# Down products of a seven-product block multiplication in another order, with partial sums left in PSUM

## The chip, the cores and the metric

The kernel runs on one core of one Trainium2 chip. The time is device microseconds of one execution: 2502.7 us, the median of three runs (2497.94 to 2503.45).

## The reference

Two request groups of 1024 tokens pass through the same one-layer trunk, with shared weights, one group ("trunk 0", "trunk 1") after the other. All inputs and outputs are float32.

```python
xn = rms_norm(h, norm_mix_g[l])
proj = xn @ w_in[l]                       # attention and recurrent branch
...
h = h + jnp.concatenate([attn_o, lru_o], axis=-1) @ w_out[l]
xn = rms_norm(h, norm_ffn_g[l])
g, u = jnp.split(xn @ w_gate_up[l], 2, axis=-1)
h = h + (jax.nn.silu(g) * u) @ w_down[l]  # hidden 2816, model 1024
h = rms_norm(h, final_norm_g)
```

The change is in how `(silu(g) * u) @ w_down` is computed and added to `h`.

## The kernel before

**Seven products.** The down product is a 2x2 block multiplication done with seven block products instead of eight. A[i,j] are blocks of the activation: i is the parity of a block of 128 tokens, j the parity of a block of 128 hidden channels. B[j,l] are blocks of `w_down`: j as above, l the half of the 1024 output columns. Each product P1 to P7 multiplies a sum of A blocks by a sum of B blocks; each result goes, with a sign, into one or more of the four blocks (i,l) of the residual `h`, by the table `C`.

**Phases and chunks.** The order of products is the tuple `DN` (L36). A product runs over NC = 11 chunks c of 256 hidden channels; here a product with its 11 chunks is called a phase, and one chunk a unit. `dn_unit` (L1933) issues a unit's matmuls: for four groups q of 128 token pairs, three matmuls of 128x512 (`mm3`, L428), since each float32 operand is split into a high and a low part. So a unit has 12 matmuls, a phase 132, the down stage of a trunk 77 units and 924 matmuls, all on TensorE (PE). The four results of a phase lie in four PSUM banks; two sets of four alternate (`bank(n % 2, ...)`). When a phase is over, its additions into `h` (VectorE, DVE, one bank and one block each) are queued and issued between the matmuls of the next phase, evenly; in P3, two to a unit.

**Preparing a unit.** `prep_dn` (L1717) forms the sums of A and B in place on DVE or GpSimd (POOL), and ScalarE (ACT) then writes the high parts of both operands, `sop` from A and `top` from B. `prep_dn_lo` (L1755) writes the low parts, that of B on DVE, that of A on POOL. Operand tiles come from a ring of seven (`wop` in profile and order). `prep` (L1780) is called ahead of each unit: it prepares units so that at most three are out, and `lows` writes the low parts of this unit and the next. Each engine works its own instructions in the order in which they are issued.

**Where the data is.** The A blocks are stored to DRAM (`ad`) by the gate-up stage and come back by `a_load` in the hook of the last gate-up tile (`gu_hook`, L1883), into the tiles aA, aB, aC, aD, aS and aV. Tile aA and parts of aB hold the block of the first phase. aC holds A[2,2] and aD A[2,1], eight of 11 chunks in one DMA of 2 MB each; the other three chunks of each lie in aB and aS. The same hook loads `h` (eight DMAs of 512 KB) and the tiles `trun` (blocks B[1,1], all 11 chunks). All other B blocks come as pieces `wraw` through a ring of four slots: the list `items` (from L1641) gives their order, and `load` (L1655) issues item i only once the units of item i-4 have been prepared (`freed`). All of these DMAs are issued by SyncE (SP), one after the other, in program order, and each waits for its slot to be free and for an earlier DMA.

Of the kernel before, what the change touches and what calls it, by code (L numbers as in the profile page):

```python
# [12 lines left out]
ALU = mybir.AluOpType  # L13
# [3 lines left out]
P = 128  # L17
# [15 lines left out]


GU = (("P1", "B11"), ("P6", "T2"), ("P2", "B21"), ("P7", "T3"), ("P5", "T1"), ("P4", "T4"), ("P3", "B22"))
DN = ("P1", "P2", "P4", "P5", "P7", "P6", "P3")  # L36
NC = NHT // 2

GELU_A = 0.044715
# [205 lines left out]
def hymba_kernel(ctx, tc, ins, outs, dbg=None):  # L245
# [1366 lines left out]
    def ffn_stream(T, b):  # L1612
# [10 lines left out]
        raws = {}  # L1623
# [3 lines left out]
        A = T.A = {}  # L1627

        def rows(t, cs, n=1):
            return wdn[t * P:(t + n) * P, cs]  # L1630
# [10 lines left out]
        def two(p, j, cs):  # L1641
            for c in range(0, NC, 2):
                items.append(((p, c), [P, 2, 512], [
                    (lambda r, i=i: r[:, i], rows(2 * (c + i) + j, cs)) for i in range(min(2, NC - c))]))

        two("P2", 1, L0)
        for c in range(NC):
            items.append((("P4", c), [P, 2, 512], [(lambda r, i=i: r[:, i], rows(2 * c + i, L1)) for i in range(2)]))
        for c in range(NC):
            items.append((("P5", c), [P, 2, 512], [(lambda r: r.rearrange("p a b -> p (a b)"), rows(2 * c, slice(0, D)))]))  # L1650
        two("P6", 0, L0)
        two("P3", 1, L1)
        freed = set()

# [61 lines left out]

        def prep_dn(p, c):  # L1717
            tr = trun[c // 2][:, c % 2]
            turn = (dve, pool)[c % 2]
            if p == "P1":  # L1720
                src, s = tr, A[1, 1, c]
            elif p == "P2":
                src, s = raws[(p, c - c % 2)][:, c % 2], A[1, 2, c]
                dve.tensor_tensor(tr, tr, src, ALU.subtract)
            elif p == "P4":
                r = raws[(p, c)]
                b12, b22 = r[:, 0], r[:, 1]
                dve.tensor_tensor(b22, b22, b12, ALU.subtract)
                turn.tensor_tensor(b12, b22, tr, ALU.add)
                src, s = b12, A[2, 2, c]  # L1730
            elif p == "P5":
                r = raws[(p, c)]
                dve.tensor_tensor(A[2, 2, c], A[2, 1, c], A[2, 2, c], ALU.add)
                dve.tensor_tensor(r[:, 0], r[:, 1], r[:, 0], ALU.subtract)
                src, s = r[:, 0], A[2, 2, c]
            elif p == "P7":
                dve.tensor_tensor(A[2, 1, c], A[1, 1, c], A[2, 1, c], ALU.subtract)
                src, s = tr, A[2, 1, c]
                dve.tensor_tensor(A[1, 1, c], A[2, 2, c], A[1, 1, c], ALU.subtract)
            elif p == "P6":  # L1740
                r = raws[(p, c - c % 2)]
                dve.tensor_tensor(tr, tr, r[:, c % 2], ALU.add)
                src, s = tr, A[1, 1, c]
            else:
                src, s = raws[(p, c - c % 2)][:, c % 2], A[1, 2, c]
            sop, top = op_tile(), op_tile()
            act.copy(sop[:, 0], s)
            act.copy(top[:, 0], src)
            if p == "P4":
                act.copy(tr, r[:, 1])  # L1750
            if p == "P6":
                turn.tensor_tensor(A[1, 2, c], A[1, 2, c], A[1, 1, c], ALU.subtract)
            half[p, c] = src, s, sop, top

        def prep_dn_lo(p, c):  # L1755
            src, s, sop, top = half.pop((p, c))
            dve.tensor_tensor(top[:, 1], src, fv(top[:, 0]), ALU.subtract)
            pool.tensor_tensor(sop[:, 1], s, fv(sop[:, 0]), ALU.subtract)
            ops["dn", p, c] = (q4((sop[:, 0], sop[:, 1])), (top[:, 0], top[:, 1]))
            if p in ("P2", "P6", "P3"):  # L1760
                if c % 2 or c == NC - 1:
                    freed.add((p, c - c % 2))
            elif p in ("P4", "P5"):
                freed.add((p, c))

        n_lo = [0]

# [32 lines left out]
    def ffn(T, b, nxt):  # L1800
# [82 lines left out]
        def gu_hook(p, t):  # L1883

            if t == last - 1 and p == "P7":
                T.trun_tile(0)
            if t < last:
                return
            if p == "P1":
                a_load(1, 1, 0, slot(xb[0], [P, 8, 512], name="aA"), 0, 8)  # L1890
                T.trun_tile(2)
            elif p == "P6":
                hold["B"] = slot(xb[1], [P, 8, 512], name="aB")
                a_load(1, 1, 8, hold["B"], 0, 2)
            elif p == "P2":
                hold["C"] = slot(xa[0], [P, 8, 512], name="aC")
                T.trun_tile(4)
            elif p == "P7":
                hold["D"] = slot(xa[1], [P, 8, 512], name="aD")
            elif p == "P5":  # L1900
                v4 = slot("V", [P, 4, 512], name="aV")
                w, s7 = (slot(x, [P, 2, 512], name="aS") for x in (f"wl{b}", "s7"))
                hold["V"] = v4
                a_load(1, 2, 0, w, 0, 2)
                a_load(1, 2, 2, s7, 0, 2)
            elif p == "P3":
                for c in (6, 8, 10):
                    T.trun_tile(c)
                a_load(1, 1, 10, hold["B"], 2, 1)
                k4, s5 = (slot(x, [P, 2, 512], name="aS") for x in (S_K, "s5"))  # L1910
                a_load(1, 2, 4, k4, 0, 2)
                a_load(1, 2, 6, s5, 0, 1)
                a_load(1, 2, 7, hold["V"], 0, 4)
                h = T.h = slot("H", [P, TT, D], name="h")
                for t_ in range(TT):
                    sync.dma_start(out=h[:, t_, :], in_=T.hd[:, t_, :])
                a_load(2, 2, 0, hold["C"], 0, 8)
                a_load(2, 2, 8, hold["B"], 3, 3)
                a_load(2, 1, 0, hold["D"], 0, 8)
                a_load(2, 1, 8, hold["B"], 6, 2)  # L1920
                a_load(2, 1, 10, s5, 1, 1)

        C = {"P1": ((1, 1, 1), (1, 2, 1), (2, 1, 1), (2, 2, 1)), "P2": ((1, 1, 1),), "P3": ((1, 2, 1),),
             "P4": ((2, 1, -1),), "P5": ((1, 2, 1), (2, 2, 1)), "P6": ((1, 2, 1), (2, 1, 1), (2, 2, 1)),
             "P7": ((2, 1, 1), (2, 2, 1))}
        adds = []
        banks = {}

# [97 lines left out]
        def before_prep(u):  # L2026
            if u in guards:
                if u == units[cur[0]]:
                    need(*guards[u])
                elif T.x_in[guards[u][0]] < guards[u][1]:  # L2030
                    return False
            if u[0] == "dn" and u[1] == "P1":
                return (1, 1, u[2]) in A
            if nxt is not None and u[0] == "dn":
                if u[1:] == ("P6", NC - 3):
# [125 lines left out]
```

## Time and profile before

| | us |
|---|---|
| median of three runs | 2502.7 |
| profiled execution | 2502.41 |
| its span | 2500.6 |
| down stage of trunk 0, first matmul to the end of the seventh phase | 1017.7 to 1259.1 |
| down stage of trunk 1 | 2255.4 to 2486.2 |

The profile is of one execution; its times count from the start of its span, and 1.8 us lie outside the span. A matmul record has a modelled end, so a phase's length is best taken from the start of its first matmul to that of the next phase. In trunk 0 the seventh phase also holds the transposes of the next trunk's input, in trunk 1 it holds down matmuls alone. The shares of busy time on the page are means over stages with different limits; the rows below are those of the down stage.

### The profile page before, as it was taken

How to read it: one execution, taken by the hardware profiler on the slowest of the kernel's cores; microseconds unless marked ns; L12 is line 12 of the kernel's file. 1: busy time of each engine (PE TensorE's matmuls, PEld its weight loads, DVE VectorE, ACT ScalarE, POOL GpSimd, SP SyncE). 2: the span in 40 equal slices, each digit the busy share in tenths (PEclk: the TensorE clock that was granted, in tenths of full speed). 3: DMA queues.
4: the chain of work that ended last, by engine and by line, in shares of the span. 5: the costliest groups of instructions: out<-in, count | busy, mean ns of one | idle time of the engine just before them, and what ended most of it. 6: DMA issues, size and time to landing. Idle time of an engine off the chain costs nothing. (4 is left out here: it accounts for less than half of the span.)

```text
span 2500.6 us, 34045 instructions
## 1 busy us (share of the span) xinstructions
PE 2357.3 (94%) x12402; PEld 1992.9 (80%) x12402; DVE 1790.1 (72%) x2480; ACT 1188.8 (48%) x2131; POOL 1262.2 (50%) x1156
## 2 busy tenths in 40 slices
PE   7998999988999999999988989999799999999997
PEld 7887899877888888777777789988678888887765
DVE  6686888876555555599966778888765555556996
ACT  4476667654232222343545776666542223224434
POOL 5323766644444444465663157665444444444665
PEclk9999999998999999999999989999999999999999
DMA  5113000111223222842430130001122222237413
GB/s 140 39 36 103 18 18 18 43 68 43 85 77 92 76 77 93 328 151 76 144 129 22 36 103 26 10 18 43 68 68 76 76 85 83 86 123 298 168 48 114
DMA packets 189704, 212.78 MB, mean 85 GB/s; under 512 B 24272, under 2 KB 141008, under 8 KB 188512
## 3 DMA queue, kind: packets, MB, share of 16 engines
q1 hardware_dynamic: 189536, 210.60, 25.8%
q8 instruction: 98, 1.61, 0.3%
q14 instruction: 70, 0.57, 0.1%
HBM read 168.45 MB, written 39.85 MB: 83 GB/s over the span
## 5 line engine op out<-in xcount | busy, mean ns | idle before, releaser
L118 PE MATMUL dn<-wop 128*128 128x512 f32 x1848 | 449.6, 401 | 18.3 <-DVE wop L118 14.7
L118 PEld LDWEIGHTS dn<-wop 128*128 128x128 f32 x1848 | 343.5, 189 | 117.6 <-DVE wop L118 36.9
L118 PE MATMUL gu<-xT,wop 128*128 128x512 f32 x1408 | 371.3, 394 | 0.0
L118 POOL TENSOR_TENSOR pexp<-pexp,rsum 128x1024 f32<-128x1024 f32 x128 | 242.9, 1898 | 228.7 <-DVE rsum L118 148.5
L118 POOL TENSOR_TENSOR wop<-wraw,wop 128x512 fp32r<-128x512 f32 x176 | 230.6, 1311 | 217.5 <-ACT wop L118 217.5
L118 PEld LDWEIGHTS gu<-xT,wop 128*128 128x128 f32 x1408 | 264.2, 188 | 59.2
L118 POOL TENSOR_TENSOR wop<-wsum,wop 128x512 fp32r<-128x512 f32 x132 | 171.7, 1301 | 266.9 <-ACT wop L118 266.9
L118 PE MATMUL gu<-xB,wop 128*128 128x512 f32 x1056 | 265.1, 398 | 3.0 <-DVE xB L118 3.0
L118 ACT CAST wop<-wraw 128x512 fp32r<-128x512 f32 x264 | 162.6, 616 | 215.4 <-DVE wraw L118 134.2
L118 PE MATMUL gu<-xH,wop 128*128 128x512 f32 x1056 | 254.7, 397 | 1.7 <-DVE act L118 1.7
L118 PEld LDWEIGHTS gu<-xH,wop 128*128 128x128 f32 x1056 | 198.8, 188 | 50.3 <-issue 2.5
L118 PEld LDWEIGHTS gu<-xB,wop 128*128 128x128 f32 x1056 | 199.3, 190 | 48.8 <-DVE xB L118 3.6
L118 ACT CAST pt<-ptp 128x512 fp32r<-128x512 f32 x256 | 148.9, 586 | 120.1 <-PE ptp L118 118.9
L118 DVE TENSOR_REDUCE m<-S 128x1 f32<-128x1041 f32 x128 | 158.1, 1235 | 55.6 <-PE S L118 54.8
L118 ACT ACTIVATE pexp<-S,m 128x1041 f32<-128x1041 f32 x128 | 145.1, 1133 | 66.9 <-DVE m L118 60.0
L118 DVE TENSOR_TENSOR pt<-ptp,pt 128x512 fp32r<-128x512 f32 x256 | 168.2, 681 | 5.4 <-ACT pt L118 4.4
L118 PE MATMUL ptp<-idf,pexp 128*128 128x128 f32 x1024 | 156.4, 277 | 10.2 <-DVE pt L118 6.7
L118 PE MATMUL pvo<-pt,vst 128*128 128x256 f32 x1024 | 156.5, 297 | 2.9 <-DVE attnT L118 2.9
L118 PE MATMUL S<-kh,qs 128*128 128x348 f32 (+1 forms) x384 | 136.9, 359 | 21.3 <-ACT pexp L118 14.9
L118 ACT CAST wop<-wsum 128x512 fp32r<-128x512 f32 x132 | 81.8, 620 | 141.9 <-DVE wsum L118 141.9
L118 DVE SCALAR_TENSOR_TENSOR act<-th,act 128x512 f32<-128x512 f32 x88 | 143.7, 1633 | 3.0
L118 PEld LDWEIGHTS ptp<-idf,pexp 128*128 128x128 f32 x1024 | 125.9, 143 | 21.3 <-issue 7.8
(289 smaller groups left out, 5189.2 us busy)
## 6 DMA issues: line engine op xcount, KB each, us to landing
wraw<-in_w_gate_up SPq DMA_DIRECT2D x176, 256.0 KB, 3.6
wraw<-in_w_down SPq DMA_DIRECT2D x110, 256.0 KB, 2.9
ad<-act SPq DMA_DIRECT2D x44, 512.0 KB, 3.5
wraw<-in_w_down SPq DMA_DIRECT2D x22, 512.0 KB, 3.3
wraw<-in_w_in SPq DMA_DIRECT2D x32, 256.0 KB, 3.4
hd<-h SPq DMA_DIRECT2D x16, 512.0 KB, 5.0
h<-hd SPq DMA_DIRECT2D x16, 512.0 KB, 10.3
out<-h SPq DMA_DIRECT2D x15, 512.0 KB, 2.6
```

The source lines that it names most:

```text
L118: return fn(*args, **kw)
```

## The change

The order of the phases becomes P2, P1, P4, P6, P5, P7, P3. P6 adds to the banks of P1, P7 to those of P6, P3 to those of P5 (`onto`), without clearing them, so that a sum of two or three products leaves PSUM in one addition. By the new table `C` there are 8 additions for each q, 32 a trunk, where there were 14 and 56. The sums of blocks are formed in other places, two to a unit in P1, P4, P6, P5 and P7, none in P2 and P3, all on DVE; POOL forms none. The block B[2,1] is loaded a second time for P1, and B[1,1] for P7. In the hook, A[1,2] takes the place of A[1,1] and the other way round; the tiles and the order of the hook's DMAs stay.

```diff
-DN = ("P1", "P2", "P4", "P5", "P7", "P6", "P3")
+DN = ("P2", "P1", "P4", "P6", "P5", "P7", "P3")
...
         two("P2", 1, L0)
+        two("P1", 1, L0)
         for c in range(NC):
             items.append((("P4", c), ...
+        two("P6", 0, L0)
         for c in range(NC):
             items.append((("P5", c), ...
-        two("P6", 0, L0)
+        two("P7", 0, L0)
         two("P3", 1, L1)
...
-            if p == "P1":
+            if p == "P2":
+                src, s = rc, A[1, 2, c]
+            elif p == "P1":
                 src, s = tr, A[1, 1, c]
-            elif p == "P2":
-                src, s = raws[(p, c - c % 2)][:, c % 2], A[1, 2, c]
-                dve.tensor_tensor(tr, tr, src, ALU.subtract)
+                dve.tensor_tensor(A[2, 1, c], A[2, 1, c], A[2, 2, c], ALU.add)
             elif p == "P4":
-                r = raws[(p, c)]
                 b12, b22 = r[:, 0], r[:, 1]
                 dve.tensor_tensor(b22, b22, b12, ALU.subtract)
-                turn.tensor_tensor(b12, b22, tr, ALU.add)
+                dve.tensor_tensor(b12, b22, tr, ALU.add)
                 src, s = b12, A[2, 2, c]
+            elif p == "P6":
+                dve.tensor_tensor(A[1, 1, c], A[2, 1, c], A[1, 1, c], ALU.subtract)
+                dve.tensor_tensor(tr, tr, rc, ALU.add)
+                src, s = tr, A[1, 1, c]
             elif p == "P5":
-                r = raws[(p, c)]
-                dve.tensor_tensor(A[2, 2, c], A[2, 1, c], A[2, 2, c], ALU.add)
                 dve.tensor_tensor(r[:, 0], r[:, 1], r[:, 0], ALU.subtract)
-                src, s = r[:, 0], A[2, 2, c]
+                dve.tensor_tensor(A[2, 2, c], A[2, 2, c], A[1, 1, c], ALU.subtract)
+                src, s = r[:, 0], A[2, 1, c]
             elif p == "P7":
-                dve.tensor_tensor(A[2, 1, c], A[1, 1, c], A[2, 1, c], ALU.subtract)
-                src, s = tr, A[2, 1, c]
-                dve.tensor_tensor(A[1, 1, c], A[2, 2, c], A[1, 1, c], ALU.subtract)
-            elif p == "P6":
-                r = raws[(p, c - c % 2)]
-                dve.tensor_tensor(tr, tr, r[:, c % 2], ALU.add)
-                src, s = tr, A[1, 1, c]
+                dve.tensor_tensor(rc, tr, rc, ALU.subtract)
+                dve.tensor_tensor(A[1, 1, c], A[1, 2, c], A[1, 1, c], ALU.subtract)
+                src, s = rc, A[2, 2, c]
...
-            if p == "P6":
-                turn.tensor_tensor(A[1, 2, c], A[1, 2, c], A[1, 1, c], ALU.subtract)
...
+            if p == "P1":
+                dve.tensor_tensor(src, src, raws[(p, c - c % 2)][:, c % 2], ALU.subtract)
...
-        C = {"P1": ((1, 1, 1), (1, 2, 1), (2, 1, 1), (2, 2, 1)), "P2": ((1, 1, 1),), "P3": ((1, 2, 1),),
-             "P4": ((2, 1, -1),), "P5": ((1, 2, 1), (2, 2, 1)), "P6": ((1, 2, 1), (2, 1, 1), (2, 2, 1)),
-             "P7": ((2, 1, 1), (2, 2, 1))}
+        C = {"P2": ((1, 1, 1),), "P1": ((1, 1, 1),), "P4": ((2, 1, -1),), "P6": ((1, 2, 1),), "P5": ((2, 2, 1),),
+             "P7": ((2, 1, 1), (2, 2, 1)), "P3": ((1, 2, 1),)}
+        onto = ("P6", "P7", "P3")
...
-                banks[n] = [bank(n % 2, q, "dn") for q in range(4)]
+                banks[n] = banks[n - 2] if p in onto else [bank(n % 2, q, "dn") for q in range(4)]
...
-                mm3(banks[n][q], sh[:, q], sl[:, q], th, tl, c == 0, c == NC - 1)
+                mm3(banks[n][q], sh[:, q], sl[:, q], th, tl, c == 0 and p not in onto, c == NC - 1, p in onto)
```

The code that issues the loads of one trunk runs on SP. This is the end of its row of DMAs for the down stage, from the hook's last two on (`ad_2155` is the stored activation of trunk 0; 128x512 is a piece of 256 KB):

```order
 L95 DMA aB<-ad_2155 128x1024
 L95 DMA aS<-ad_2155 128x512
-L95 DMA wraw<-in_w_down 128x512 x25
+L95 DMA wraw<-in_w_down 128x512 x47
 L95 DMA wraw<-in_w_down 128x1024 x11
 L95 DMA wraw<-in_w_down 128x512 x19
```

Behind the hook's last load stand 25 pieces before and 47 now; in both the first three are chunks 8, 9 and 10 of P2, then follow, now, the 11 of P1, in both the 22 of P4, and, now, the 11 of P6.

ScalarE writes the high parts. These are the casts of chunks 7 to 10 of the first phase of trunk 0, before, which is P1 (aA, aB: A block; trun_9280, trun_9283 and trun_9286: chunks 6 and 7, 8 and 9, and 10 of B[1,1]):

```order
L118 CAST wop_9403<-trun_9280 128x512
L118 CAST wop_9420<-aB_9182 128x512
L118 CAST wop_9421<-trun_9283 128x512
L118 CAST wop_9438<-aB_9182 128x512
L118 CAST wop_9439<-trun_9283 128x512
L118 CAST wop_9456<-aB_9182 128x512
L118 CAST wop_9457<-trun_9286 128x512
```

The same place of the change, where the first phase is P2 (wraw_9165: chunks 6 and 7, in the fourth slot; wraw_9314: chunks 8 and 9, in the slot that chunks 0 and 1 had; wraw_9357: chunk 10):

```order
L118 CAST wop_9411<-wraw_9165 128x512
L118 CAST wop_9428<-aB_9182 128x512
L118 CAST wop_9429<-wraw_9314 128x512
L118 CAST wop_9449<-aB_9182 128x512
L118 CAST wop_9450<-wraw_9314 128x512
L118 CAST wop_9467<-aB_9182 128x512
L118 CAST wop_9468<-wraw_9357 128x512
```

The B operands of chunks 8 to 10 of the first phase come from the ring of four slots now, no longer from `trun`.

VectorE at the end of the first phase, before (the low parts of chunks 7 to 10 of P1, then P2; the sums of P2 on trun are mixed in):

```order
L118 TENSOR_TENSOR wop_9403<-trun_9280,wop_9403 128x512
L118 TENSOR_TENSOR wop_9421<-trun_9283,wop_9421 128x512
L118 TENSOR_TENSOR wop_9439<-trun_9283,wop_9439 128x512
L118 TENSOR_TENSOR trun_9075<-trun_9075,wraw_8960 128x512
L118 TENSOR_TENSOR wop_9457<-trun_9286,wop_9457 128x512
```

The same place of the change (the low parts of chunks 7 to 10 of P2, then P1):

```order
L118 TENSOR_TENSOR wop_9411<-wraw_9165,wop_9411 128x512
L118 TENSOR_TENSOR wop_9429<-wraw_9314,wop_9429 128x512
L118 TENSOR_TENSOR wop_9450<-wraw_9314,wop_9450 128x512
L118 TENSOR_TENSOR aD_9221<-aD_9221,aC_9199 128x512
L118 TENSOR_TENSOR wop_9468<-wraw_9357,wop_9468 128x512
L118 TENSOR_TENSOR aD_9221<-aD_9221,aC_9199 128x512
L118 TENSOR_TENSOR wop_9490<-trun_9075,wop_9490 128x512
L118 TENSOR_TENSOR trun_9075<-trun_9075,wraw_9395 128x512
```

The sums of aD and aC, which the first phase before did not touch, stand ahead of the low part of chunk 10 of the first phase; from there on each unit of P1 has two sums and a low part, where P2 before had one sum and a low part.

## Rows read from the trace of the kernel before

**Rows 1.** Page, part 1: busy time, share of span, instructions.

```profile
PE 2357.3 (94%) x12402; PEld 1992.9 (80%) x12402; DVE 1790.1 (72%) x2480; ACT 1188.8 (48%) x2131; POOL 1262.2 (50%) x1156
```

**Rows 2.** Windows by down phase: P4, P5, P7, P6, P3 of trunk 1; last P4 to P6, trunk 0.

```profile
core 0: us, PE busy (x) PEld busy (x) DVE busy (x) ACT busy (x) POOL busy (x), PEclk, DMA share, GB/s
2319.41:2352.33 32.92, 31.43 (x133) 24.59 (x132) 32.78 (x33) 16.74 (x30) 23.77 (x15) 1.00 0.48 160
2352.33:2384.21 31.88, 31.88 (x134) 24.06 (x132) 31.81 (x38) 13.43 (x23) 16.57 (x12) 1.00 0.54 181
2384.21:2419.59 35.38, 33.34 (x133) 24.00 (x132) 35.07 (x41) 13.08 (x24) 22.88 (x14) 1.00 0.01 2
2419.59:2455.58 35.99, 32.46 (x134) 24.15 (x133) 34.67 (x37) 12.79 (x23) 22.36 (x16) 1.00 0.23 82
2455.58:2486.20 30.62, 30.62 (x133) 24.64 (x131) 17.64 (x22) 15.29 (x35) 15.74 (x19) 1.00 0.20 73
1083.19:1218.65 135.46, 130.17 (x530) 97.93 (x528) 133.07 (x144) 55.73 (x96) 84.57 (x53) 0.99 0.33 112
```

**Rows 3.** Windows, down matmuls alone: first eight chunks of trunk 1, of trunk 0.

```profile
2255.40:2280.46 25.06, 22.52 (x96) 17.98 (x96) 0.00 (x0) 1.00 0.83 307
1017.73:1044.33 26.60, 24.03 (x97) 19.11 (x96) 0.00 (x0) 0.94 0.84 310
```

**Rows 4.** SyncE's DMA issues, timeline: start, us; trunk 1, then trunk 0.

```profile
2265.11 8.54 SPq L95 DMA_DIRECT2D h<-hd  x8
...
2277.16 0.32 SPq L95 DMA_DIRECT2D aD<-ad  x1
...
2280.84 0.32 SPq L95 DMA_DIRECT2D aS<-ad  x1
2287.65 48.32 SPq L95 DMA_DIRECT2D wraw<-in_w_down  x25
...
1039.50 0.32 SPq L95 DMA_DIRECT2D aD<-ad  x1
...
1042.06 0.32 SPq L95 DMA_DIRECT2D aS<-ad  x1
```

**Rows 5.** DMA issues of trunk 1: KB each, us to landing.

```profile
aD<-ad SPq DMA_DIRECT2D x1, 2048.0 KB, 19.2
...
aS<-ad SPq DMA_DIRECT2D x1, 256.0 KB, 17.5
...
wraw<-in_w_down SPq DMA_DIRECT2D x2, 256.0 KB, 11.4
```

**Rows 6.** The same two of trunk 0.

```profile
aD<-ad SPq DMA_DIRECT2D x1, 2048.0 KB, 18.3
...
aS<-ad SPq DMA_DIRECT2D x1, 256.0 KB, 17.7
```

**Rows 7.** Page, part 6: DMA issues over the whole span.

```profile
wraw<-in_w_down SPq DMA_DIRECT2D x110, 256.0 KB, 2.9
```

**Rows 8.** ScalarE timeline, chunk 9 of the first phase, trunk 1.

```profile
2277.92 0.62 ACT L118 CAST wop<-trun 128x512 fp32r<-128x512 f32 x1 [1.60 <-POOL wop L118]
```

**Rows 9.** VectorE timeline in the preparation of P5 and P7, trunk 1.

```profile
2346.43 1.79 DVE L118 TENSOR_TENSOR aC<-aD,aC 128x512 f32<-128x512 f32 x1
2348.15 0.68 DVE L118 TENSOR_TENSOR wraw<-wraw 128x512 f32<-128x512 f32 x1
2348.75 0.68 DVE L118 TENSOR_TENSOR wop<-wraw,wop 128x512 fp32r<-128x512 f32 x1
2349.35 1.78 DVE L118 TENSOR_TENSOR aC<-aD,aC 128x512 f32<-128x512 f32 x1
...
2355.17 0.67 DVE L118 TENSOR_TENSOR h<-h,dn 128x512 f32<-128x512 f32 x1
```

**Rows 10.** Windows on TensorE behind two waits in front of the gate-up stage.

```profile
1806.20:1809.20 3.00, 2.93 (x13) 0.50 0.00 0
1817.30:1821.50 4.20, 4.20 (x13) 0.50 0.00 0
```

More of the change, by code (lines that the diff above doesn't have):

```diff
@@ L1718, in prep_dn @@
             tr = trun[c // 2][:, c % 2]
-            turn = (dve, pool)[c % 2]
-            if p == "P1":
+            r = raws[(p, c if p in ("P4", "P5") else c - c % 2)]
+            rc = r[:, c % 2]
+            if p == "P2":
+                src, s = rc, A[1, 2, c]
+            elif p == "P1":
                 src, s = tr, A[1, 1, c]
-            elif p == "P2":
-                src, s = raws[(p, c - c % 2)][:, c % 2], A[1, 2, c]
-                dve.tensor_tensor(tr, tr, src, ALU.subtract)
+                dve.tensor_tensor(A[2, 1, c], A[2, 1, c], A[2, 2, c], ALU.add)
             elif p == "P4":
-                r = raws[(p, c)]
                 b12, b22 = r[:, 0], r[:, 1]
                 dve.tensor_tensor(b22, b22, b12, ALU.subtract)
-                turn.tensor_tensor(b12, b22, tr, ALU.add)
+                dve.tensor_tensor(b12, b22, tr, ALU.add)
                 src, s = b12, A[2, 2, c]
+            elif p == "P6":
+                dve.tensor_tensor(A[1, 1, c], A[2, 1, c], A[1, 1, c], ALU.subtract)
+                dve.tensor_tensor(tr, tr, rc, ALU.add)
+                src, s = tr, A[1, 1, c]
             elif p == "P5":
-                r = raws[(p, c)]
-                dve.tensor_tensor(A[2, 2, c], A[2, 1, c], A[2, 2, c], ALU.add)
                 dve.tensor_tensor(r[:, 0], r[:, 1], r[:, 0], ALU.subtract)
-                src, s = r[:, 0], A[2, 2, c]
+                dve.tensor_tensor(A[2, 2, c], A[2, 2, c], A[1, 1, c], ALU.subtract)
+                src, s = r[:, 0], A[2, 1, c]
             elif p == "P7":
-                dve.tensor_tensor(A[2, 1, c], A[1, 1, c], A[2, 1, c], ALU.subtract)
-                src, s = tr, A[2, 1, c]
-                dve.tensor_tensor(A[1, 1, c], A[2, 2, c], A[1, 1, c], ALU.subtract)
-            elif p == "P6":
-                r = raws[(p, c - c % 2)]
-                dve.tensor_tensor(tr, tr, r[:, c % 2], ALU.add)
-                src, s = tr, A[1, 1, c]
+                dve.tensor_tensor(rc, tr, rc, ALU.subtract)
+                dve.tensor_tensor(A[1, 1, c], A[1, 2, c], A[1, 1, c], ALU.subtract)
+                src, s = rc, A[2, 2, c]
             else:
-                src, s = raws[(p, c - c % 2)][:, c % 2], A[1, 2, c]
+                src, s = rc, A[1, 1, c]
             sop, top = op_tile(), op_tile()
@@ L1759, in prep_dn_lo @@
             ops["dn", p, c] = (q4((sop[:, 0], sop[:, 1])), (top[:, 0], top[:, 1]))
[L1760 to L1763, printed above, removed]
+            if p == "P1":
+                dve.tensor_tensor(src, src, raws[(p, c - c % 2)][:, c % 2], ALU.subtract)
+            if p in ("P4", "P5"):
                 freed.add((p, c))
+            elif c % 2 or c == NC - 1:
+                freed.add((p, c - c % 2))
         n_lo = [0]
@@ L1889, in gu_hook @@
             if p == "P1":
-                a_load(1, 1, 0, slot(xb[0], [P, 8, 512], name="aA"), 0, 8)
+                a_load(1, 2, 0, slot(xb[0], [P, 8, 512], name="aA"), 0, 8)
                 T.trun_tile(2)
@@ L1893, in gu_hook @@
                 hold["B"] = slot(xb[1], [P, 8, 512], name="aB")
-                a_load(1, 1, 8, hold["B"], 0, 2)
+                a_load(1, 2, 8, hold["B"], 0, 2)
             elif p == "P2":
@@ L1903, in gu_hook @@
                 hold["V"] = v4
-                a_load(1, 2, 0, w, 0, 2)
-                a_load(1, 2, 2, s7, 0, 2)
+                a_load(1, 1, 0, w, 0, 2)
+                a_load(1, 1, 2, s7, 0, 2)
             elif p == "P3":
@@ L1908, in gu_hook @@
                     T.trun_tile(c)
-                a_load(1, 1, 10, hold["B"], 2, 1)
+                a_load(1, 2, 10, hold["B"], 2, 1)
                 k4, s5 = (slot(x, [P, 2, 512], name="aS") for x in (S_K, "s5"))
-                a_load(1, 2, 4, k4, 0, 2)
-                a_load(1, 2, 6, s5, 0, 1)
-                a_load(1, 2, 7, hold["V"], 0, 4)
+                a_load(1, 1, 4, k4, 0, 2)
+                a_load(1, 1, 6, s5, 0, 1)
+                a_load(1, 1, 7, hold["V"], 0, 4)
                 h = T.h = slot("H", [P, TT, D], name="h")
@@ L2031, in before_prep @@
                     return False
-            if u[0] == "dn" and u[1] == "P1":
-                return (1, 1, u[2]) in A
+            if u[0] == "dn" and u[1] == "P2":
+                return (1, 2, u[2]) in A
             if nxt is not None and u[0] == "dn":
-                if u[1:] == ("P6", NC - 3):
+                if u[1:] == ("P7", NC - 3):
                     T.no_rope = True
```

## Prediction

> **What bounds the kernel now.** I read the page first: TensorE is busy for 94% of the span [rows 1], so nothing is won except where it waits. Then I cut the down stage into its phases with the windows view. The last phase, P3, shows what TensorE alone needs: 132 matmuls in 30.6 us, 2.78 us a unit, with VectorE busy for 17.6 us. In P4, P5, P7 and P6 VectorE is busy for nearly the whole of each window, and the phases last 32.9, 31.9, 35.4 and 36.0 us, 136.2 us in trunk 1 where four full-rate phases would take 122.5; in trunk 0 they take 135.5 [rows 2]. So 13.7 and 13.0 us are to be had from VectorE, 26.7 us or 1.1% of the span. That is all the relief that there is.
>
> Why VectorE is full at so few instructions shows in its timeline. In the preparation of P5 a unit has three sums with both inputs in SBUF, issued 0.60 us apart when nothing interferes (2348.15, 2348.75, 2349.35), but the first of each unit lasts 1.78 us and the pattern repeats every 2.92 us. In that time POOL writes the low part of A. An addition into `h`, which reads PSUM, lasts 0.67 us [rows 9]. The 2.92 us are three times 0.60 and 1.12 us of standing still.
>
> The third view is the queue of loads at the head of the stage. SP issues eight loads of `h` from 2265.1 on, then the A blocks; aD leaves at 2277.16, and the last, aS, at 2280.84 [rows 4]. They take 19.2 and 17.5 us to land, at 2296.4 and 2298.3, and a `wraw` piece issued at 2287.65 takes 11.4 us, to 2299.05 [rows 4, 5]. Over the span such a piece takes 2.9 us [rows 7]. So for about 30 us the loads land in the order of issue and anything issued behind aS lands behind it. Before, nobody needs one of those pieces for a long while: the first phase reads its B blocks from `trun`, which is issued ahead of `h`, and P2 comes a phase later.
>
> **Part 1: P2 goes first, with its B blocks in the ring.** The ring has four slots of two chunks each. Chunks 0 to 7 of P2 are loaded before the stage. Chunks 8, 9 and 10 need a slot that a chunk of P2 itself frees, so their loads come in the program behind the hook, and SP issues them behind aS. The order of SP shows them there, the order of ScalarE shows that the high part of chunk 8 is now cast from such a piece.
>
> When is chunk 8 wanted? In trunk 1 its first matmul starts at 2280.46, the end of a window that holds the 96 matmuls of eight chunks; in trunk 0 at 1044.33 [rows 3]. I take these as the planned starts, since nothing ahead of them changes in kind. When is it there? SP's turn comes just behind aS, about 1.2 us later (eight loads in 8.54 us, rows 4), but the piece lands behind aS: 0.7 us later, as the piece did that was issued at 2287.65, so at 2299.0. In trunk 0 aS lands at 1042.06 + 17.7 = 1059.8 [rows 4, 6], the piece at 1060.5. Then ScalarE casts it, 0.62 us [rows 8], and VectorE forms the low part, 0.68 us [rows 9], with about 0.1 us for the hand-overs; the second matmul of the unit needs the low part, 0.2 us after its start. So:
>
> - trunk 1: 2299.0 + 1.4 - (2280.5 + 0.2) = 19.7 us of waiting;
> - trunk 0: 1060.5 + 1.4 - (1044.3 + 0.2) = 17.4 us.
>
> Nothing covers this: behind the blocked cast on ScalarE are the casts of chunks 9 and 10 and of all of P1, VectorE has the low part of chunk 8 in front, and TensorE runs the units in order. The sum is 37.1 us. Bounds: 0 if the piece overtook everything, 40 if chunk 9's piece also counts.
>
> **Part 2: the clock after it.** Behind two waits ahead of the gate-up stage TensorE worked at a granted clock of 0.50, the lower level of 1.2 GHz, for 3.0 and 4.2 us [rows 10]. Half of such a stretch is lost. I take 2 us for each of the two stops, 4 us; bounds 0 and 8.
>
> **Part 3: the additions.** The table gives 32 instead of 56 a trunk, and the order of VectorE counts 64 for both; I reckon with that and not with 36. 24 times 0.6 us goes from VectorE a trunk, 14 us, but those instructions read PSUM and can lie in the time that POOL keeps the others standing [rows 9]. The eight of P7 lie in P3, which has room.
>
> **Part 4: the sums.** Before, P2 had one sum a unit on VectorE, P4 and P6 one and a half (the other half on POOL), P5 and P7 two. Now P1, P4, P6, P5 and P7 have two, all on VectorE, and each unit still has its low part and POOL's. That is the mix of P5 before, which cost 2.92 us a unit in the timeline and 31.9 us in the phase [rows 2, 9]. P7 before had the same count with one sum waiting for the other on the same block, and its phase took 35.4 us, of which I put 2 us down to the change-over to P6. P1 (a sum on `trun` behind the low part that reads it) and P4 (two sums in a row on one block) are of that kind: 33 us. So 3 x 31.9 + 2 x 33 = 161.7 us for five phases that took 136.2 + 30.6 = 166.8 us: a gain of 5.1 in trunk 1, and of 4.4 in trunk 0, 9.5 together. Bounds: five phases at P6's 36.0 us would be a loss of 13 us a trunk; at the full 30.6 us a gain of 13.8.
>
> The Trainium skill has this as a rule (SBUF — State Buffer, "SBUF: two separate sides"): VectorE with two SBUF inputs and GpSimd reading SBUF hold one port pair in turn, each for its whole instruction. By that rule VectorE must add POOL's time to its own, which is the 2.92 us above and agrees with the 1.78 us rows; without it three instructions of 0.68 us fit into 2.78 us, the five phases run at full rate and the gain is 26.7 us. The rule speaks against the change, since it trades additions from PSUM for sums in SBUF.
>
> **Part 5: the rest.** The second loads of B[2,1] and B[1,1] are 2.8 MB each over phases in which the DMA share is 0.54 or less [rows 2]: nothing. The accumulating phases start on banks whose additions were issued in the first units of the phase between: nothing, unless VectorE falls a whole phase behind. In trunk 0 the next trunk's transposes may start two units earlier; between 0 and 3 us gained, I take 0.
>
> **Sum.** 2502.4 (profiled execution, 0.3 below the median) + 37.1 + 4 - 9.5 = 2534.
>
> **Rivals.**
>
> *The pieces overtake, and a second wait shows.* A small piece might land long before a large DMA issued ahead of it. For it: the 2.9 us of such a piece over the span [rows 7]; against it: its 11.4 us here, and that all loads of rows 5 land in the order of issue. Then it lands 1.2 + 2.9 us behind aS's issue, at 2284.9 and 1046.2, and chunk 8 waits 5.6 and 3.1 us. But now the first sum of P1, on aD and aC, stands on VectorE ahead of the low part of chunk 10, and aD lands only at 2296.4 and 1057.8 [rows 4 to 6]. A sum and a low part later, 1.4 us, chunk 10 can run: 2297.8 and 1059.2, against 2291.9 and 1053.2 by its turn. That is 5.9 and 6.0 us. Together 20.6 + 4 - 9.5: 2517.5 us. The Trainium skill (DMA: Bandwidth & Descriptors, "Queues, rings and completion order") says that completion is not first-in-first-out for one issuing engine, which would allow this; the landings here are in order.
>
> *VectorE's relief decides.* Place: the five phases; price: 9.5 us gained, 26.7 at most. It decides if chunk 8 and aD are late by less than 4.8 us a trunk, that is if the pieces were issued ahead of `h` or the A blocks landed 15 us sooner. The order of SP speaks against the first, the landings against the second. Time: 2493 us, 2476 at best; faster.
>
> *The new mix is dearer than P5.* If each unit ran at P6's pace, five phases would take 180 us: 13 us lost a trunk instead of 5 gained, 2570 us. For it: three in-place chains a unit in P1. Against it: P6's extra time goes with POOL's sums, which are gone.
>
> **How the numbers follow.** The waiting for the pieces: 0.78. Overtaking with the second wait: 0.10. VectorE's relief: 0.06. The dearer mix: 0.06. The first case by itself spans 2519 (33 us of waiting, 2 of clock, 18 gained) to 2548 (40, 6, 0); with the second case the range is 2514 to 2549. About 0.2%, 5 us, is what a measurement can tell from no change; faster than that 0.05, within it 0.03, slower 0.92.
>
> **What would show it.** Right: in both trunks one gap of 17 to 20 us on down matmuls after the 96th, put down to ScalarE's or VectorE's `wop` or to the DMA of `wraw`; the first piece behind aS landing at the same time as before although issued 5 us sooner; a low clock just behind the gap; P6 and P5 near 31.9 us, and no change-over stall from P7. Wrong: a piece that lands in under 5 us there, a gap at chunk 10 instead, or phases of 30.6 us throughout.

## The result, and the profile after

| | us |
|---|---|
| predicted | 2534 (2514 to 2549) |
| measured after | 2537.35, median of four runs (2535.70 to 2537.93) |
| before, on the same chip | 2500.32, median of four runs (2494.90 to 2503.45) |
| ratio | 1.0151, 95% interval 1.0136 to 1.0166 |

The change is slower by 37 us. The profiled execution after has a span of 2536.0 us, against 2500.6 before: 35.4 us more, which is what the traces have to explain. TensorE does the same work, as the page's first part shows in its busy time and count (beside [rows 1]); it waits more. The profile before is of an execution 2.1 us above the median of its four, so a difference of 2 or 3 us in one stretch of the ledger below can be that of two executions.

```profile
PE 2358.2 (93%) x12402; PEld 1995.0 (79%) x12402; DVE 1793.1 (71%) x2474; ACT 1187.9 (47%) x2131; POOL 1230.7 (49%) x1136
```

The windows view, cut at the phase starts of the kernel after: first P2 of trunk 0 and its next five phases together, then P2, P1, P4, P6, P5, P7 and P3 of trunk 1. The columns are those of [rows 2].

```profile
1014.71:1068.50 53.79, 34.58 (x133) 26.95 (x132) 19.84 (x19) 13.30 (x24) 17.68 (x12) 0.81 0.83 318
1068.50:1233.91 165.41, 158.25 (x662) 122.09 (x660) 160.45 (x183) 69.15 (x120) 83.25 (x55) 1.00 0.38 125
2270.73:2326.63 55.90, 35.91 (x133) 27.82 (x132) 20.67 (x20) 13.33 (x24) 17.09 (x12) 0.79 0.80 305
2326.63:2357.39 30.76, 30.76 (x134) 24.74 (x132) 30.38 (x35) 11.95 (x21) 15.33 (x10) 1.00 0.25 85
2357.39:2392.06 34.67, 32.43 (x133) 24.27 (x132) 34.36 (x40) 18.59 (x33) 17.79 (x11) 1.00 0.54 176
2392.06:2426.71 34.65, 32.63 (x133) 25.27 (x132) 34.65 (x39) 13.99 (x23) 18.89 (x13) 0.96 0.28 93
2426.71:2458.85 32.14, 31.24 (x134) 24.93 (x132) 32.14 (x38) 12.57 (x22) 15.65 (x11) 0.99 0.52 171
2458.85:2491.90 33.05, 31.68 (x133) 24.44 (x132) 30.12 (x35) 12.57 (x22) 17.02 (x12) 1.00 0.27 89
2491.90:2523.40 31.50, 30.90 (x133) 24.55 (x131) 19.57 (x21) 15.36 (x36) 17.50 (x20) 1.00 0.24 91
```

The same windows before, first P1 and the next five phases together of trunk 0, then of trunk 1:

```profile
1017.73:1052.68 34.95, 32.38 (x133) 25.88 (x132) 19.59 (x21) 13.51 (x24) 16.31 (x12) 0.95 0.89 339
1052.68:1218.65 165.97, 160.68 (x662) 122.77 (x660) 160.34 (x181) 69.33 (x120) 99.64 (x64) 0.99 0.37 126
2255.40:2288.82 33.42, 30.88 (x134) 24.75 (x133) 19.63 (x21) 13.53 (x24) 16.32 (x12) 1.00 0.88 338
2288.82:2455.58 166.76, 159.70 (x662) 121.63 (x661) 161.66 (x181) 69.65 (x121) 100.66 (x65) 1.00 0.35 122
```

The first row of each trunk is the loss: P2 takes 53.79 and 55.90 us where the first phase before, P1, took 34.95 and 33.42. In the windows of P2 TensorE is busy for only 35 us and VectorE for 20. The next five phases have VectorE nearly full, as before. The ledger of the whole span:

| stretch | before | after | difference |
|---|---|---|---|
| first phase, trunk 0 and 1 | 34.95 + 33.42 | 53.79 + 55.90 | +41.3 |
| the next five, trunk 0 and 1 | 166.0 + 166.8 | 165.4 + 165.3 | -2.1 |
| P3, trunk 0 and 1 | 40.4 + 30.6 | 42.6 + 31.5 | +3.1 |
| ahead of trunk 0's down stage | 1017.7 | 1014.7 | -3.0 |
| between the two down stages | 996.4 | 994.2 | -2.2 |
| behind the last | 14.4 | 12.6 | -1.8 |

The timeline of TensorE, trunk 1 (in brackets the idle time ahead, and what ended it), shows where in P2 the time is:

```profile
2276.45 21.15 PE L118 MATMUL dn<-wop 128*128 128x512 f32 x83 [2.54 <-DVE wop L118]
2315.05 42.73 PE L118 MATMUL dn<-wop 128*128 128x512 f32 x169 [17.45 <-ACT wop L118]
```

There are 13 down matmuls ahead of the first row, so the gap of 17.45 us stands behind the 96th, ahead of chunk 8. In trunk 0 the same gap is 16.64 us. The chain of waits through it, in order of time, which is best read backwards from the matmul:

```profile
2285.35 11.99 DMA h<-hd
...
2297.40 16.88 DMA wraw<-in_w_down
...
2314.38 0.63 ACT wop L118
...
2315.05 8.97 PE dn L118 x24
```

ScalarE's cast waits for the piece of B, which takes 16.88 us to land, and the piece's own issue waited for one of the `h` loads to land. SyncE's own timeline gives the queue (the column behind the start is the time over which it issued):

```profile
2280.51 8.32 SPq L95 DMA_DIRECT2D h<-hd  x8
...
2294.91 0.32 SPq L95 DMA_DIRECT2D aS<-ad  x1
2297.40 37.03 SPq L95 DMA_DIRECT2D wraw<-in_w_down  x14
```

The piece leaves 2.49 us behind aS and lands 0.7 us behind it: aS took 18.7 us to landing, to 2313.6, and the piece this, to 2314.28:

```profile
wraw<-in_w_down SPq DMA_DIRECT2D x1, 256.0 KB, 16.9
```

Such a piece took 2.9 us over the span before [rows 7]. When it was issued, two loads of `h`, aC, aD and the three small loads beside them had not landed, 6.8 MB; with the piece's own 0.26 MB, 7.1 MB in 16.9 us are about 419 GB/s. The DMA view counts 406 GB/s for the queue from 2292 to 2293 us.

The windows behind the two gaps, TensorE alone (busy time, count, granted clock, DMA share, GB/s), show what a gap leaves behind:

```profile
2315.05:2321.51 6.46, 6.46 (x15) 0.50 0.40 140
1058.09:1061.99 3.90, 3.90 (x9) 0.50 0.64 234
```

TensorE works at 0.50 of its clock there, the lower of its two levels. Chunk 8 lasts 5.59 and 4.81 us instead of 2.78, and in trunk 1 chunk 9 takes 3.21.

### The profile page after: what moved, and what is told of

Same layout as the page of the kernel before. It is cut to its first block, busy times and chain, and to the rows that moved or that the text cites. A ratio compares the mean times of both kernels' runs of the same rounds, so it can differ in the third digit from the quotient of the medians.

```text
span 2536.0 us, 34064 instructions
## 1 busy us (share of the span) xinstructions
PE 2358.2 (93%) x12402; PEld 1995.0 (79%) x12402; DVE 1793.1 (71%) x2474; ACT 1187.9 (47%) x2131; POOL 1230.7 (49%) x1136
## 4 chain that ended last, share of the span: by engine, by line
PE 59%; DVE 24%; ACT 6%; issue 4%; DMA 4%; POOL 3%; SPq 0%; DVEq 0%; POOLq 0%; ACTq 0%
PE gu L118 33%; PE op L118 5%; PE S L118 4%; PE pvo L118 4%; DVE wop L118 4%; PE ptp L118 3%; ACT arena L118 3%; DVE wraw L118 2%; PE dn L118 2%; DVE arena L118 2%; DVE h L118 2%; PE qp L118 1%; DMA wraw<-in_w_down 1%; DVE m L118 1%; DVE aS L118 1%
## 5 line engine op out<-in xcount | busy, mean ns | idle before, releaser
L118 PE MATMUL dn<-wop 128*128 128x512 f32 x1848 | 454.1, 404 | 55.4 <-ACT wop L118 34.4
L118 PEld LDWEIGHTS dn<-wop 128*128 128x128 f32 x1848 | 348.8, 192 | 153.7 <-DVE wop L118 40.8
L118 ACT CAST wop<-wraw 128x512 fp32r<-128x512 f32 x286 | 176.1, 616 | 327.2 <-DVE wraw L118 233.4
L118 DVE TENSOR_TENSOR wop<-wraw,wop 128x512 fp32r<-128x512 f32 x110 | 99.5, 908 | 82.7 <-ACT wop L118 82.7
```

The source lines that it names most:

```text
L118: return fn(*args, **kw)
```

## The experiments

Two questions were open: whether the wait is the bytes ahead of the piece, and where the relief of VectorE went. The executions of one kernel spread by 5 to 12 us, so each ratio is taken from all of them, and a trace shows one. Kernels are compared with the kernel before on the same chips (2496.6 us for the first four below, 2497.9 for the others).

**The same loads with `h` behind the pieces.** Only the place of the eight `h` loads changes; they are needed by the first addition, a phase later. The order of blocks is turned to match the additions.

```diff
-                h = T.h = slot("H", [P, TT, D], name="h")
-                for t_ in range(TT):
-                    sync.dma_start(out=h[:, t_, :], in_=T.hd[:, t_, :])
...
+        def h_load():
+            h = T.h = slot("H", [P, TT, D], name="h")
+            for t_ in (0, 2, 4, 6, 1, 3, 5, 7):
+                sync.dma_start(out=h[:, t_, :], in_=T.hd[:, t_, :])
+
         def dn_unit(p, c):
             n = DN.index(p)
+            if (p, c) == ("P2", 6):
+                h_load()
```

> The changed kernel with the eight loads of h (4.2 MB) issued in the seventh unit of P2, behind the late pieces of P2 and four pieces of P1, instead of in the hook. Theory (loads land in the order of issue; the late pieces wait for the bytes ahead of them): 4.2 MB at 406 GB/s are 10.3 us, so the pieces of chunk 8 land 10.3 us sooner and the wait in front of chunk 8 shrinks from 16.6 and 17.5 us to 6 and 7; aD lands in time for chunk 10; in all about 21 us less, 2516 us. Rival (the wait comes from the slots of the ring or from the new order of products): the wait stays at 17 us, 2537 us. Rival (pieces land on their own, bytes ahead don't matter): no change either.

Measured: 2514.62 us (2510.02 to 2522.33), ratio 1.0064 (1.0045 to 1.0084), near the 2516 expected. TensorE's timeline, trunk 1:

```profile
2299.86 20.36 PE L118 MATMUL dn<-wop 128*128 128x512 f32 x77 [8.85 <-ACT wop L118]
```

The gap halves, to 8.85 us here and 7.29 in trunk 0. The piece still takes 18.1 us from issue to landing, but it lands 33.31 us after the stage's first matmul instead of 43.55. Taking 4.2 MB out of the queue ahead of it brought it forward by 10.2 us; at the 406 GB/s that the queue moved in the kernel after, 4.2 MB are 10.3 us. The landing is a matter of bytes ahead.

**Chunks 8 to 10 of P2 from `trun`.** The hook loads B[2,1], the block of P2, for these three chunks into the `trun` tiles, and their B[1,1], first used in P1, is loaded once the low part has read them. No piece of P2 is left behind `h`.

```diff
-        two("P2", 1, L0)
+        for c in range(0, 8, 2):
+            items.append((("P2", c), [P, 2, 512], [
+                (lambda r, i=i: r[:, i], rows(2 * (c + i) + 1, L0)) for i in range(2)]))
...
-                    sync.dma_start(out=trun[c // 2][:, i], in_=rows(2 * (c + i), L0))
+                    sync.dma_start(out=trun[c // 2][:, i], in_=rows(2 * (c + i) + (c >= 8), L0))
...
-            r = raws[(p, c if p in ("P4", "P5") else c - c % 2)]
+            r = trun[c // 2] if p == "P2" and c >= 8 else raws[(p, c if p in ("P4", "P5") else c - c % 2)]
...
+            if p == "P2" and c >= 8:
+                sync.dma_start(out=src, in_=rows(2 * c, L0))
```

> The changed kernel with chunks 8 to 10 of P2 read from the trun tiles, which the hook loads ahead of h, and B[1,1] of these chunks loaded into them afterwards; everything else as changed. Theory (two waits lie one behind the other, the second hidden by the first): no wait at chunk 8; a wait of 9 to 12 us at chunk 10, whose low part stands on VectorE behind the first sum on aD and aC; 39.7 us go, 21 and some 3 for the clock come back, 2521 us. Rival (only the late pieces of P2 cost time): no wait in P2 at all, 2498 us.

Measured: 2517.32 us (2511.71 to 2522.34), ratio 1.0081 (1.0061 to 1.0100). Chunk 8 no longer waits. The gap stands two units later, behind the first matmul of chunk 10, TensorE in trunk 1:

```profile
2266.72 25.30 PE L118 MATMUL dn<-wop 128*128 128x512 f32 x108 [2.54 <-DVE wop L118]
2302.72 35.33 PE L118 MATMUL dn<-wop 128*128 128x512 f32 x144 [10.70 <-DVE wop L118]
```

VectorE's timeline says why: the sum for P1 stands ahead of chunk 10's low part and waits for aD.

```profile
2301.38 0.69 DVE L118 TENSOR_TENSOR aD<-aD,aC 128x512 f32<-128x512 f32 x1 [16.51 <-DMA aD<-ad]
2301.98 0.68 DVE L118 TENSOR_TENSOR wop<-trun,wop 128x512 fp32r<-128x512 f32 x1
```

So behind the wait for the pieces lies a second one, for aD, 10.70 us here and 8.80 in trunk 0. The kernel after hides it: chunk 8 is later than aD there (aD lands at 2311.6, the piece at 2314.28).

**Loads in the order of need.** `h` late as above, and the 2 MB loads of aC and aD issued in the hooks of the units P7 and P5 of the last gate-up tile, ahead of the other loads of that tile's last hook.

```diff
             elif p == "P7":
                 hold["D"] = slot(xa[1], [P, 8, 512], name="aD")
+                a_load(2, 2, 0, hold["C"], 0, 8)
             elif p == "P5":
...
+                a_load(2, 1, 0, hold["D"], 0, 8)
             elif p == "P3":
...
-                a_load(2, 2, 0, hold["C"], 0, 8)
...
-                a_load(2, 1, 0, hold["D"], 0, 8)
```

> The changed kernel with the loads in the order of need: aC issued behind unit P7 and aD behind unit P5 of the last gate-up tile, h in the seventh unit of P2 as in e1. Theory (order of loads is all that makes the change slow): pieces of chunk 8 land before 2280 in the time of the kernel before, no wait at chunk 8 or 10, both P2 phases near 35 us as the first phase before; 2537 - 40 = 2498 us, the same as before within 0.3%. Rival (the new order of products costs something of its own, 10 us or more): 2508 us or above.

Measured: 2504.01 us (2499.19 to 2508.35), ratio 1.0022 (1.0012 to 1.0033); 6 us above what was expected. A gap of 4.93 us at chunk 8 remains in trunk 1 (in trunk 0 that unit starts 4.0 late). SyncE's timeline shows where the time goes:

```profile
2256.79 9.79 SPq L95 DMA_DIRECT2D trun<-in_w_down  x5
```

Five issues that take 3.1 us in the kernel after and in the one with `h` late take 9.79 here, and the load behind them goes out 14.4 us into the stage instead of 7.8. The chain of waits says why the fifth stands still: it goes out at 2266.25, as soon as the store of the last A tile has landed, and that store, the first line, took 10.00 us, where in the kernel after, the second line, it took 3.35.

```profile
2256.23 10.00 DMA ad<-act
```

```profile
2274.75 3.35 DMA ad<-act
```

The store was issued 7.5 us behind the 2 MB load of aD, which landed 1.3 us ahead of it (2248.76, 2264.97). That the load held the store up is read from this order and was not tested. Even without the long wait the change is no faster than before: the five phases last 165.1 and 165.3 us, as in the kernel after.

**The low part of A on VectorE.** The same kernel with one word changed: 77 instructions a trunk go from POOL to VectorE, which was busy for 161.5 of the 165.1 us of trunk 1's five phases.

```diff
-            pool.tensor_tensor(sop[:, 1], s, fv(sop[:, 0]), ALU.subtract)
+            dve.tensor_tensor(sop[:, 1], s, fv(sop[:, 0]), ALU.subtract)
```

> e3 with the low part of the A operand formed on VectorE instead of GpSimd, in all seven phases. Theory (in the phases with two sums VectorE's instructions on SBUF stand still while GpSimd works on SBUF: 3 x 0.6 + 1.12 us a unit): VectorE has 4 x 0.6 = 2.4 us and its additions to do, under the 2.78 us of TensorE, and nothing to stand still for; the five phases fall from 165 to about 154 us a trunk, 22 us less than e3, about 2476 us. Rival (VectorE is simply full, at 0.7 to 1.8 us an instruction): one more instruction a unit makes the five phases 0.6 us a unit longer, 66 us more than e3, 2560 us.

Measured: 2476.59 us (2474.22 to 2478.90), ratio 0.9917 (0.9903 to 0.9932). The windows of the five phases of trunk 1, first with POOL, then without:

```profile
2293.24:2458.31 165.07, 157.99 (x662) 122.25 (x661) 161.47 (x183) 69.67 (x121) 84.68 (x56) 1.00 0.37 130
```

```profile
2280.12:2433.12 153.00, 153.00 (x661) 124.00 (x660) 144.61 (x237) 69.00 (x121) 0.00 (x0) 1.00 0.40 140
```

VectorE does 54 instructions more in 17 us less, and TensorE never waits: 153.00 of 153.00 us. So 84.7 us of POOL's work had cost VectorE far more than the 54 instructions by themselves. The groups of instructions in these windows say which of them it held up, a sum in SBUF and the additions into `h` (behind the bar busy time and mean ns; first with POOL, then without):

```profile
L118 DVE TENSOR_TENSOR wraw<-wraw 128x512 f32<-128x512 f32 x22 | 22.5, 1024 | 0.0
...
L118 DVE TENSOR_TENSOR h<-h,dn 128x512 f32<-128x512 f32 x22 | 14.8, 676 | 0.0
```

```profile
L118 DVE TENSOR_TENSOR wraw<-wraw 128x512 f32<-128x512 f32 x22 | 15.1, 685 | 0.0
L118 DVE TENSOR_TENSOR h<-h,dn 128x512 f32<-128x512 f32 x22 | 14.9, 680 | 0.0
```

This settles the mechanism of rows 9: VectorE's sums stand still while POOL works, its additions don't.

**The additions doubled.** The kernel with loads in the order of need, every addition but P3's done twice, so that its output is not the reference's.

```diff
-                    for i, l, sign in C[p]:
+                    for i, l, sign in C[p] * (1 if p == "P3" else 2):
```

> e3 with every addition into h of P2, P1, P4, P6, P5 and P7 done twice, 60 instead of 32 a trunk; the sum in h is then another than the reference's. Theory (additions read PSUM and lie in the time in which GpSimd keeps VectorE's other instructions standing, or in phases with room): within 4 us of e3, 2504 to 2508 us. Rival (VectorE is full in five phases, so each addition is 0.6 us on the path; the change gains by dropping 24 of them): 24 x 0.6 = 14 us a trunk, P3's being free, 2532 us.

Measured: 2532.13 us (2527.89 to 2536.11), ratio 1.0134 (1.0119 to 1.0148). The total is the rival's, but its place is not. The windows of the five phases of trunk 1:

```profile
2310.69:2481.08 170.39, 160.57 (x661) 121.62 (x660) 168.40 (x203) 69.55 (x121) 80.63 (x56) 1.00 0.36 127
```

Twenty additions more (203 VectorE instructions for 183) lengthen them by 5.3 us, and by 5.2 in trunk 0: 0.27 us each on average, less than half of the 0.60 us pitch. Each phase has four of them, and the phases differ: P4 grows by 2.25 us, nearly the pitch of four instructions, and P6 not at all (33.14 us for 33.36). The other eight lie in P3, which isn't longer (30.6 us for 31.5). Another 14.3 us stand between the two down stages, where nothing was edited: 1006.1 us for 991.8, with TensorE at the granted clock of 0.50 for 64.9 us there instead of 47.8. That isn't the chance of one execution, since the mean granted clock of the four was 0.972 or 0.973 and that of the twelve without the edit 0.976 to 0.980; why the stretch moves was not tested. So an addition costs neither nothing nor its length.

**The kernel before with the low part of A on VectorE.** The one-word edit in the kernel before, its 56 additions kept.

> The kernel before the change with the low part of the A operand formed on VectorE instead of GpSimd; 56 additions a trunk as before. Theory (VectorE and GpSimd on SBUF take turns, and that alone makes P4, P5, P7 and P6 slow): the four phases fall from 136 and 135.5 us to 123 to 126, about 24 us less than before, 2473 us, although VectorE gets 77 more instructions a trunk and keeps its 56 additions. Rival (the number of additions is the bound): no gain or a loss of up to 0.6 us a unit, 2500 to 2550 us.

Measured: 2472.58 us (2470.72 to 2475.41), ratio 0.9897 (0.9883 to 0.9910). Windows of P4, P5, P7 and P6 of trunk 1, as in [rows 2], of which P4 and P7 stand here:

```profile
2301.14:2331.86 30.72, 30.72 (x134) 24.73 (x132) 30.58 (x44) 17.14 (x31) 6.19 (x4) 1.00 0.50 176
...
2362.41:2398.40 35.99, 32.26 (x133) 24.25 (x132) 35.71 (x52) 12.70 (x23) 6.57 (x4) 1.00 0.03 11
```

Three of the four run at TensorE's pace (P5 and P6 take 30.55 and 30.57 us). P7 doesn't: there VectorE is full at 35.71 us, with 52 instructions and four sums of POOL beside them. VectorE's timeline at one of these:

```profile
2372.97 0.68 DVE L118 TENSOR_TENSOR wop<-trun,wop 128x512 fp32r<-128x512 f32 x1
2373.57 1.76 DVE L118 TENSOR_TENSOR wop<-aD,wop 128x512 fp32r<-128x512 f32 x1
```

POOL's timeline at the same time:

```profile
2373.13 1.65 POOL L118 TENSOR_TENSOR aS<-aS,aA 128x512 f32<-128x512 f32 x1 [5.69 <-DVE aA L118]
```

52 instructions at the 0.60 us pitch are 31.2 us, and four such holds of 1.1 us make 35.6. Of the phases with sums this is the one in which fewer additions and sums without POOL have something to win.

**All loads in the order of need.** `h` late, aC and aD early, and chunks 8 to 10 of P2 from `trun`; POOL keeps its low parts.

> e3 and e2 together: loads in the order of need and chunks 8 to 10 of P2 in the trun tiles. Theory (the waits at chunks 8 and 10 are all that the change loses, its phases gain 1 to 2 us a trunk): e3 loses its waits of 3.8 and 4.9 us and the slow matmuls behind them, 14 us together, 2490 us; against the kernel before 0 to 7 us faster. Rival (something else in the new order costs 5 us or more): 2497 us or above.

Measured: 2496.79 us (2495.94 to 2503.26), ratio 1.0002 (0.9994 to 1.0011). No gap is left in P2 (33.4 and 35.0 us). The down stages last 239.7 and 230.8 us, before 241.3 and 230.8. So the new order of products, freed of its late loads, gains 1.6 us in one trunk and nothing in the other. The kernel is 7 us above the 2490 expected, at the edge of the rival's range; its stretch between the stages is 8.1 us longer than in the kernel without the edit on `trun` (999.9 for 991.8), again with 64.9 us at the lower clock.

**The same with the low part of A on VectorE.** Both edits together.

> e7 with the low part of the A operand on VectorE: the change without its two costs. Theory: e5 without its waits of 4.6 and 6.5 us at chunk 8 and the slow matmuls behind them, 16 us less than e5, 2460 us; every unit of the down stage of trunk 1 at 2.78 us but the second. Rival (the waits at chunk 8 in e5 cover something else that comes out now): 2468 us or more.

Measured: 2465.30 us (2464.78 to 2471.39), ratio 0.9866 (0.9851 to 0.9881), the fastest of all. Windows of P2, P1, P4, P6, P5 and P7 of trunk 1, of which P6 and P7 stand here:

```profile
2335.41:2365.97 30.56, 30.56 (x134) 24.81 (x132) 30.51 (x52) 13.37 (x22) 0.00 (x0) 1.00 0.29 100
...
2396.61:2427.19 30.58, 30.58 (x134) 24.80 (x133) 25.74 (x44) 12.57 (x22) 0.00 (x0) 1.00 0.27 96
```

P6 has 52 VectorE instructions, as many as P7 of the kernel before with the same edit, and without POOL runs at TensorE's pace; P7 has 44 and takes 30.58 us instead of 35.99. The down stages last 222.7 and 216.9 us, against 227.1 and 220.8 there: with POOL's hold gone the change is worth 4 us a trunk. How much of that the kernel before would also gain if the four sums of POOL beside its P7 went to VectorE was not tested.

The time is 5 us above the 2460 expected and below the rival's 2468. Not every unit keeps 2.78 us, as it should have: P1 of trunk 1 takes 31.80 us. The two down stages are 15.0 us shorter than with the loads in the order of need and the same word changed, where 16 were expected; the rest lies elsewhere, and the traced execution, at 2471.39 us the slowest of the four, can't place it.

## Why the prediction was right, and where it was not

The forecast was 2534, the time 2537.35, the side and the cause as forecast. Point by point:

**Part 1, the waits at chunk 8: right.** In trunk 1 the cast was forecast 43.7 us after the stage's first matmul (2299.1 to 2255.4); it came after 43.65 (2314.38 to 2270.73). Chunk 8 starts 17.6 us late where 19.7 were forecast, and in trunk 0 16.8 where 17.4 were: its turn in trunk 1 came 1.6 us later than planned, since unit 1 took 7.15 us instead of 5.56. The test with `h` late shows that bytes ahead set it. The Trainium skill's statement that completion is not first-in-first-out for one issuing engine (DMA: Bandwidth & Descriptors, "Queues, rings and completion order") didn't help the piece here: it landed 0.7 us behind aS, as forecast.

**Part 2, the clock: right, a little small.** 2 us for each stop were forecast; the chunks behind the gap last 2.0 us longer in trunk 0 and 3.2 in trunk 1, with the clock at 0.50 for 3.9 and 6.5 us. The second window of rows 10 had also ended too soon: there the clock stayed at 0.50 for 5.6 us behind the wait, not 4.2. Parts 1 and 2 together were 41.1 us, and the ledger's first row has +41.3; so close a sum is luck, for it is made of about 34.4 us of waiting instead of 37.1, 5.2 of clock instead of 4, and the 1.6 us of unit 1 that no term had.

**Part 3, the additions: the count right, the price half wrong.** "Those instructions read PSUM and can lie in the time that POOL keeps the others standing" holds in part: by the doubling they cost nothing in P6, 0.56 us each in P4, and 0.27 on average.

**Part 4, the sums: the step that failed.** Five phases were forecast to gain 9.5 us in both trunks; they gained 2.1. The term "P1 and P4 ... are of that kind: 33 us" and the 31.9 us for P6, P5 and P7 were measured so:

| phase | forecast | trunk 0 | trunk 1 |
|---|---|---|---|
| P1 | 33 | 32.15 | 30.76 |
| P4 | 33 | 34.60 | 34.67 |
| P6 | 31.9 | 33.41 | 34.65 |
| P5 | 31.9 | 32.99 | 32.14 |
| P7 | 31.9 | 32.25 | 33.05 |

The traces show two things that the term left out. The first is what an addition does to POOL's hold. These are the held sums of P5 before on VectorE, the first two in units with an addition, the last two in units without:

```profile
2355.76 1.19 DVE L118 TENSOR_TENSOR aC<-aD,aC 128x512 f32<-128x512 f32 x1
...
2358.68 1.18 DVE L118 TENSOR_TENSOR aC<-aD,aC 128x512 f32<-128x512 f32 x1
...
2369.70 1.78 DVE L118 TENSOR_TENSOR aB<-aB 128x512 f32<-128x512 f32 x1
...
2372.61 1.78 DVE L118 TENSOR_TENSOR aB<-aB 128x512 f32<-128x512 f32 x1
```

Either unit takes 2.9 us, since the addition [rows 9] falls into the hold, of which 0.5 us are left for the sum instead of 1.1. In P4, after, most of the additions miss it. POOL's 11 low parts hold 11 VectorE instructions, as in P5 before, but nine of them by 0.9 us or more, there seven; and P4 has two instructions more (40 in its window, 38 in that of P5). Each of the two is worth about 1.2 us, of the 2.8 between the phases.

The second is the change-over stall "from P7" that was to go: it came back at P6's last unit, which lasts 6.36 us (5.07 in trunk 0). There POOL's low parts of P6 and P5 follow each other within 0.3 us, and three VectorE instructions in a row stand still, VectorE's timeline:

```profile
2417.57 1.78 DVE L118 TENSOR_TENSOR wraw<-wraw 128x512 f32<-128x512 f32 x1
2419.27 1.78 DVE L118 TENSOR_TENSOR aC<-aC,aS 128x512 f32<-128x512 f32 x1
2420.97 1.75 DVE L118 TENSOR_TENSOR wop<-trun,wop 128x512 fp32r<-128x512 f32 x1
```

POOL's timeline at the same time:

```profile
2417.27 1.52 POOL L118 TENSOR_TENSOR wop<-aV,wop 128x512 fp32r<-128x512 f32 x1 [1.39 <-issue]
2418.76 1.75 POOL L118 TENSOR_TENSOR wop<-aD,wop 128x512 fp32r<-128x512 f32 x1
2420.78 1.39 POOL L118 TENSOR_TENSOR wop<-aD,wop 128x512 fp32r<-128x512 f32 x1 [0.28 <-PE dn L118]
```

In trunk 1 TensorE's granted clock was also at 0.50 for 3.4 us at that place (2423.91 to 2427.32). P5 and P7 have one unit of 4.0 us each, in both trunks, whose cause stays open.

The mechanism behind the term was right: with POOL idle the five phases run at TensorE's pace, 12.1 us faster in trunk 1. The rule quoted with it (the Trainium skill, SBUF — State Buffer, "SBUF: two separate sides") agrees with the rows shown here: the sums are held up, the additions are not (676 and 680 ns). The prediction drew from it only that the sums are dear, not that the low part of A was on the wrong engine.

**Part 5: 0 to 3 us gained were allowed for trunk 0's P3, 0 taken.** It is 2.2 us longer, in trunk 1 0.9.

**The sum was right partly by luck.** The miss of part 4 (7.4 us) and P3's 3.1 are in large part balanced by 7.0 us gained outside the down stages, where nothing was forecast: 41.3 - 2.1 + 3.1 - 7.0 = 35.3 us, of the 35.4 in the spans. The four executions before spread by 8.6 us, so one trace of each kernel doesn't show that the 7.0 us belong to the change.

**The rivals.** The second wait, at chunk 10, is real: the rival put chunk 10 late by 5.6 + 5.9 = 11.5 and 3.1 + 6.0 = 9.1 us, and with chunk 8 supplied from `trun` it is 10.70 and 8.80. It was hidden behind the first. "VectorE's relief decides" came to nothing when the loads were put right: 2496.79 us against 2497.9 before, within the interval of no change, where the rival had 9.5 to 26.7 us less. "The new mix is dearer than P5" is true to a small part: five phases in 165.3 us, where the forecast had 161.7 and the rival 180.

## What to carry to other kernels

Before moving a stage's first step, list what its last units need and count the bytes queued ahead of it on the issuing engine. Here 7.1 MB at about 419 GB/s were the 16.9 us that a piece took whose median is 2.9, and a second late load hid behind the first. Where two engines hold each other up, count the work by what it does to the bound engine: moving POOL's share to a VectorE that was busy for 98% of a stretch made that stretch 7% shorter. A gain in one stage is only read from that stage, since other stretches of a program with the same work moved by up to 14 us between these kernels, and the executions of one kernel spread by up to 12.

## What the runs showed of the hardware that was not expected

- A full VectorE became faster by taking over work: 165.07 us with 183 instructions, 153.00 with 237.
- Five small issues of SyncE took 9.79 us, against 3.08 to 3.16 in two other kernels: the fifth waited for a store to land, which took 10.00 us, issued 7.5 us behind a 2 MB load, instead of 3.35.
- An addition from PSUM, 0.68 us long, cost 0.27 us on average in a stretch where VectorE was busy for 98%, and nothing in the phase where it fell into the time that POOL held a sum up.
- The stretch between the two down stages, with nearly the same matrix work (5150 to 5166 matmuls in the records of the six windows read), took 991.6 to 1006.1 us over the traces of the ten kernels, with TensorE at 0.50 of its clock for 44.4 to 68.3 us. The three longest, 999.9 to 1006.1, are those with over 60 us at that clock; but the kernel after has 51.2 us of it, as the kernel before, and is 2.2 us shorter. It is not the order of issue alone: of 17 executions of the kernel before on one chip, the two fastest (2493.3 and 2493.4 us) had a mean granted clock of 0.980 and the slowest (2504.0 us) 0.975. What decides it stays open.
